# An attention that loads its values from the kernel's output, in place of a second copy sorted by head

## The chip, the cores and the metric

The kernel runs on one core of a Trainium2 chip. The core has five engines with queues of their own: TensorE (PE: matmuls, and PEld for its weight loads), VectorE (DVE), ScalarE (ACT), GpSimd (POOL) and SyncE (SP), which here issues nearly all transfers. 16 DMA engines carry them. The metric is the time of one execution on the device in microseconds (us).

## The reference, cut to what matters

One inference step of a decoder with two layers: a recurrent layer (RG-LRU), then a layer of forgetting attention. Between them the keys K, the values V and a log forget value are computed once from the residual stream `x`. Two groups go through it: a prompt of 2,048 new tokens, and 8 sequences of 8 new tokens each ("sample"), which also read 4,096 past tokens from a paged cache of K and V (32 pages of 128 tokens per sequence). There are 16 heads of 64, and `D_MODEL` is 1024.

```
z = rms_norm(x, kv_norm) @ w_kv
k, v = z[..., :1024], z[..., 1024:2048]        # both are outputs of the kernel, row by row
logf = log_sigmoid(z[..., 2048:] + b_f);  c = cumsum(logf)
...
zz = rms_norm(x, b_pre_norm) @ b_w_in;   q, g = zz[..., :1024], zz[..., 1024:]
s  = q k^T / 8 + c_q - c_k, causal;   o = softmax(s) v          # per head
x  = x + rms_norm((o * silu(g)) @ b_w_out, b_post_norm)
```

All is in float32. The outputs include `v_prompt`, of shape (1, 2048, 16, 64): a token's row holds its 16 heads one after the other.

## The kernel before, in words

The recurrent layer runs in two parts of 1,024 tokens, and the projections behind it (`phase_b`) in three: 64 sample rows and 1,024 prompt tokens, then 512, then 512. `phase_b` goes through kinds and column blocks in a written order (`B_ORDER`, `B_ENDS`, `B_LAST`): "k" and "v" are computed token by token (`token_major`: one tile is 128 tokens by 256 columns, that is four heads), "q" and "g" feature by feature (`feature_major`). Each float32 matmul is made of three (L386 to L388), high and low parts multiplied with each other; the weights are split into these parts on the way in (ACT L431, DVE L432).

A "v" tile `kf` goes out twice. L928 writes its 256 columns to the output `v_p` (`vp_flat` is the same memory as 2,048 rows of 1,024). L939 writes it again to `v_d`, a scratch tensor in DRAM laid out by head: [head, 128 tokens of a tile, tile, 64]. In this copy a head's values for one partition, 16 tiles of 64 floats, are 4 KB in one piece. A profile calls the scratch tensor `vd`, the weights before the split `wst`, and the activations `xh` and `xl`; the last two are read back from DRAM for the third part (L1943, `back`).

The attention of the prompt (`attention`) takes the heads one by one and each head's queries in four blocks of 512. A tick is one block of 128 keys: a score matmul in two halves (L1653, L1654), an exponential on ACT (L1664), and every four or eight ticks a `product` of the probabilities with the values (L1677). A head has 40 ticks. At tick 16 of a head the next head's keys and values are loaded (L1407, L1411), the values into one of two tiles, `vvs[0]` and `vvs[1]`. `vvs[0]` is a tile of its own (in the profile `vvt`); `vvs[1]` is the first quarter of the memory that held the low parts of the activations (`attl`). The rest of that memory holds tiles of queries and of row sums.

Beside `phase_b` and the attention runs the decode of the sample group (`decode`): for each sequence and half of the heads (a "turn") the 32 key pages are loaded (L1138, `raw`, 256 KB each), turned on VectorE (L1210), multiplied with the queries on PE (L1194), then the softmax, then the 32 value pages and their products (L1292). `Side` lays decode and main work side by side in the program by costs written down by hand. All these loads and stores stand in the one queue of SP, in order; the order within each engine's queue is worked out when the program is built, by a scheduler that uses simulated times (`schedule_with_timeline_sim`, L2007), with some places fixed by hand (`paged`, `behind`, `together`).

After the last head the output projection (`project`) takes tiles of 128 tokens: `fetch` loads the attention's output, the reciprocals of the row sums and the gate (`sg`, [128, 8, 128]), `gate` multiplies them in two halves (PE L1746, DVE, POOL L1748), then `split`, the matmuls, and `post`. Two sets of tiles take turns; the gate tile of the first set (`sgT`) is a tile of its own, that of the second lies in memory of a key tile.

Of the kernel before, what the change touches and what calls it, by code (L numbers as in the profile page):

```python
# [20 lines left out]
P = 128  # L21
D = 1024
KB = 8
# [65 lines left out]
def tile_hawk_fox(  # L89
# [80 lines left out]
    def dt_(name, shape):  # L170
        return dram.tile(shape, F32, name=name, tag=name)
# [9 lines left out]

    kd_d, qd_d = dt_("kd", [D, 2, SEQ]), dt_("qd", [D, 2, SEQ])
    sg_d = dt_("sgd", [D, SEQ])
    v_d = dt_("vd", [H, P, SEQ // P, HD])
    nc_d = dt_("ncd", [H, 3, SEQ])
    ks_d, vs_d = dt_("ksd", [NSAMP, D]), dt_("vsd", [NSAMP, D])

# [690 lines left out]
    def phase_b(s, x, feed, nk, early, order, opening=None):  # L878
# [7 lines left out]
        with ExitStack() as es:  # L886
# [22 lines left out]
            def token_major(kind, cc):  # L909

                nonlocal forget
                W = feed.take()
                isk = kind == "k"
                kfs = []
                w = WC if (kind, cc) == ("k", 0) else 256
                for i, (col, m, samp, tok) in enumerate(s.tiles):
                    ps = mmp("kv")
                    mm3(ps[:m, :w], lambda k: xh(k, col, m), lambda k: xl(k, col, m),
                        W.h(0, w), W.l(0, w), KB)
                    kf = pool.tile([P, 256], F32, name="kf", tag="kf", bufs=nk)  # L920
                    A.copy(kf[:m, :], ps[:m, :256])  # L921
                    if w > 256:
                        tt(V, s.z[:m, i, :], ps[:m, 256:w], bfB[:m, :], ALU.add)
                        if i == nt - 1 and not early:
                            forget = logf(s, pool)
                    sl = slice(cc * 256, (cc + 1) * 256)
                    dst = (ks_flat if samp else kp_flat[tok:tok + m]) if isk else (vs_flat if samp else vp_flat[tok:tok + m])
                    S.dma_start(dst[:, sl], kf[:m, :])  # L928
                    if samp:
                        S.dma_start((ks_d if isk else vs_d)[:, sl], kf[:m, :])  # L930
                        known.add((kind, cc))
                    elif isk:
                        kfs.append((kf, tok))
                        if len(kfs) == 4 or i == nt - 1:
                            for fb in range(2):
                                later.after(2 + fb, lambda grp=kfs, cc=cc, fb=fb: keys(grp, cc, fb))
                            kfs = []
                    else:
                        S.dma_start(v_d[cc * 4:cc * 4 + 4, :, tok // P, :].rearrange("h p d -> p h d"), kf[:, :].rearrange("p (h d) -> p h d", h=4))  # L939
                    later.tick()  # L940
                    if i == nt - 1 or i == 0:
                        feed.fetch()
                        feed.fetch()
                    if i >= 1:
                        feed.split()
                        feed.fetch()
                    next(forget, None)
                    yield 24 * 109
# [417 lines left out]
    def attention(es):  # L1366
# [41 lines left out]
            heads[h] = ka  # L1408

        def load_values(h):  # L1410
            S.dma_start(vvs[h % 2][:, :, :], v_d[h])  # L1411


        def load_unit(u):
# [161 lines left out]
        room = sbuf(es, "att2")  # L1576
        kbs.append(xs2[0][:, :SEQ])
        kas.append(xs2[0][:, SEQ:])
        vvs.append(f(xs2[1][:, :1024]).rearrange("p (k d) -> p k d", k=16))
        part = [xs2[1][:, i * 512:(i + 1) * 512] for i in range(2, 8)]  # L1580
        qbs.extend(part[:3])
        lent["rr"] = part[3:5]
        qal += [part[5], room.tile([P, 512], F32R, name="qa3")]

        def ring(tiles):
            turn_ = [0]
# [134 lines left out]
    def project(es):  # L1721

        bpostB, out = proj["g"], proj["out"]

        def tiled(t):
            return t.rearrange("p (k t) -> p k t", k=KB)

        def fetch(i, og, sg):
            m, t, res, _ = rows[i]
            if t is None:  # L1730
                tt(V, og[:, :, :m], oTs[:, :, :], sgs[:, :, :], ALU.mult)
                return
            qc, at = t // 512, slice(t % 512, t % 512 + P)
            S.dma_start(og[:, :, :], og_d[qc][:, at].rearrange("(k p) t -> p k t", p=P))
            for j, rr in enumerate(lent["rr"]):
                S.dma_start(f(rr[:4, :]).rearrange("z (k t) -> z k t", k=4),
                            r_d[qc, :, :, j * 4:(j + 1) * 4, at].rearrange("x z k t -> (x z) k t"))
            S.dma_start(sg[:, :, :], sg_d[:, t:t + P].rearrange("(k p) t -> p k t", p=P))

        def gate(i, og, sg):  # L1740
            if rows[i][1] is None:
                return
            for j, rr in enumerate(lent["rr"]):
                half = slice(j * 4, (j + 1) * 4)
                ps = lent["psum"].tile([P, 512], F32, name="rp", tag="sx", bufs=3)
                T.matmul(ps[:, :], sel[:, :], rr[:, :], start=True, stop=True)  # L1746
                tt(V, og[:, half, :], og[:, half, :], ps[:, :].rearrange("p (k t) -> p k t", k=4), ALU.mult)
                tt(G, og[:, half, :], og[:, half, :], sg[:, half, :], ALU.mult)  # L1748

        def residual(i, x1):  # L1750
            m, t, res, _ = rows[i]
            S.dma_start(x1[:m, :], res)

        def split(i, og, oh, ol):
            m = rows[i][0]
            cp(A, oh[:, :, :m], og[:, :, :m])
            tt(V, ol[:, :, :m], og[:, :, :m], f(oh[:, :, :m]), ALU.subtract)

        def post(i, yps, x1, y):
            m, t, res, dst = rows[i]  # L1760
            halves_ = [slice(j * 512, (j + 1) * 512) for j in range(2)]
            if i == len(rows) - 1:
                for sl, ps in zip(halves_, yps):
                    tt(V, y[:m, sl], ps[:m, :], bpostB[:m, sl], ALU.mult)
            ss = sumsq(None, yps, m)
            r = rsqrt(ss[:m], m, 0.25 / D, post=0.5)
            for sl, ps in zip(halves_, yps):
                if i == len(rows) - 1:
                    V.scalar_tensor_tensor(y[:m, sl], y[:m, sl], r[:m, 0:1], x1[:m, sl], op0=ALU.mult, op1=ALU.add)
                    S.dma_start(dst[:, sl], y[:m, sl])  # L1770
                else:
                    V.scalar_tensor_tensor(y[:m, sl], ps[:m, :], r[:m, 0:1], bpostB[:m, sl], op0=ALU.mult, op1=ALU.mult)
                    tt(G, y[:m, sl], y[:m, sl], x1[:m, sl], ALU.add)
            if i < len(rows) - 1:
                S.dma_start(dst, y[:m, :])

        pool = sbuf(es, "proje", "right")
        hs = lent["halves"]
        sel = pool.tile([P, P], F32R, name="selz")
        G.memset(f(sel[:, :]), 0.0)  # L1780
        for z in range(2):
            tt(V, sel[:4, z * HD:(z + 1) * HD], ident[:4, z:z + 1].to_broadcast([4, HD]),
               ident[:4, z + 2:z + 3].to_broadcast([4, HD]), ALU.add)
        sets = [dict(og=pool.tile([P, KB, P], F32, name="ogT"), sg=pool.tile([P, KB, P], F32, name="sgT"), x1=proj["x1"],
                     oh=pool.tile([P, KB, P], F32R, name="ohT"), ol=pool.tile([P, KB, P], F32R, name="olT"),
                     y=proj["y"],
                     ps=lambda j: psum["dec"].tile([P, 512], F32, name="y", tag="do"[j], bufs=1)),
                dict(og=tiled(lent["og"][:, :D]), sg=tiled(lent["res"][:, :D]), x1=lent["res"][:, D:], oh=tiled(hs[:, :D]), ol=tiled(hs[:, D:]),
                     y=lent["out"][:, :, :].rearrange("p k d -> p (k d)"),
                     ps=lambda j: lent["psum"].tile([P, 512], F32, name="y", tag="st", bufs=2))]  # L1790

        def part(i, fn, *names):
            if i < len(rows):
                fn(i, *(sets[i % 2][n] for n in names))

        for i in range(2):
            part(i, fetch, "og", "sg")
            part(i, residual, "x1")
        part(0, split, "og", "oh", "ol")
        for i in range(len(rows)):  # L1800
            b = sets[i % 2]
            yps = []
            part(i + 1, gate, "og", "sg")
            for j in range(2):
                ps = b["ps"](j)
                out.product(ps, rows[i][0], j, b["oh"], b["ol"])
                yps.append(ps)
                if j == 0:
                    part(i + 2, fetch, "og", "sg")
                    part(i + 1, split, "og", "oh", "ol")  # L1810
            post(i, yps, b["x1"], b["y"])
            part(i + 2, residual, "x1")
            if i == 3:
                later.flush()
# [203 lines left out]
```

## Time and profile before

| | us |
|---|---|
| median of 3 runs | 2939.27 |
| lowest and highest run | 2931.56, 2940.05 |
| the profiled execution | 2939.13 |
| its span, first to last instruction | 2937.4 |
| PE busy in it | 2749.3 (94%) |
| busy time of q1, the queue of nearly all transfers, as a share of 16 DMA engines | 68.1% |

The profile is of one execution. A group of instructions in it is one line of the program with what it writes and reads (`vd<-kf`); "x64" is the number of instructions. A wait is told as "who <- whom: us in total, times, longest". PE's busy time includes matmuls that are slow because the clock is held back, so the granted clock (PEclk) is read beside it. For DMA, a packet is one piece that lies together at both ends, and the busy share is that of 16 engines.

### The profile page before, as it was taken

Reading aid. Unit: us, or ns where it says so; the run is one execution under the profiler, and the core shown is the slowest. Engines: PE = TensorE matmul, PEld = TensorE weight load, DVE = VectorE, ACT = ScalarE, POOL = GpSimd, SP = SyncE. Lnnn points to the kernel's source line nnn. Section 1 sums busy time; section 2 is a strip of 40 time slices with the busy share of each in tenths; the row PEclk is TensorE's granted clock in tenths of the full one; section 3 lists DMA queues with packets and bytes.
Section 4 is the critical chain, followed back from the end, with each engine's and each line's share of the span. In section 5 each row is a group of like instructions: output and inputs, shape, how many; then the busy total and the mean of one; then the engine's idle time right before and its main releaser. Section 6 shows DMA issues by size and latency. Waiting matters only on the chain.

```text
span 2937.4 us, 59474 instructions
## 1 busy us (share of the span) xinstructions
PE 2749.3 (94%) x21086; PEld 2229.5 (76%) x21086; DVE 1814.4 (62%) x3971; ACT 1266.8 (43%) x2874; POOL 1099.7 (37%) x1207
## 2 busy tenths in 40 slices
PE   5998999999999999999999999899999999999998
PEld 5997789988898997897878666556666665556687
DVE  7877456344257774776564676766766765655465
ACT  4666342222245664533342344454444444356221
POOL 1654110000014552100001175656565565559554
PEclk9999999999999999999999999999999999999999
DMA  4224536789751246699999979978889877783453
GB/s 126 82 91 132 161 125 182 220 258 307 240 159 63 79 137 187 231 302 349 322 349 319 334 253 327 304 258 284 280 287 312 285 256 261 245 276 90 125 189 130
DMA packets 488149, 654.91 MB, mean 223 GB/s; under 512 B 93752, under 2 KB 288057, under 8 KB 480380
## 3 DMA queue, kind: packets, MB, share of 16 engines
q1 hardware_dynamic: 487564, 649.01, 68.1%
q8 instruction: 167, 2.74, 0.4%
q0 software_dynamic: 288, 2.10, 0.2%
q14 instruction: 130, 1.06, 0.1%
HBM read 514.87 MB, written 135.95 MB: 222 GB/s over the span
## 4 chain that ended last, share of the span: by engine, by line
PE 60%; DMA 15%; DVE 9%; ACT 6%; SPq 5%; issue 3%; POOL 1%; DVEq 0%; ACTq 0%; POOLq 0%
PE ops L1677 8%; PE st L1653 4%; PE sx L1440 4%; PE y L386 4%; PE y L388 4%; PE y L387 4%; DMA raw<-in_cache_k_dram 4%; PE st L1654 3%; PE dO L1292 3%; PE dS L1194 3%; DMA raw<-in_cache_v_dram 3%; PE qg L388 2%; PE qg L386 2%; PE qg L387 2%; SPq L1138 2%
## 5 line engine op out<-in xcount | busy, mean ns | idle before, releaser
L1210 DVE STREAM_TRANSPOSE ktr<-raw 128x1024 f32<-128x1024 f32 x256 | 308.1, 1226 | 107.8 <-DMA raw<-in_cache_k_dram 80.0
L1442 DVE TENSOR_REDUCE mxs<-sx 128x1 f32<-128x512 f32 x384 | 254.2, 681 | 145.3 <-PE sx L1440 144.3
L386 PE MATMUL kv<-wh,xh 128*128 128x256 f32 (+3 forms) x1088 | 310.3, 289 | 11.5 <-DMA xh<-xhd 4.6
L387 PE MATMUL kv<-wl,xh 128*128 128x256 f32 (+3 forms) x1088 | 309.6, 287 | 3.1 <-DVE wl L432 3.1
L388 PE MATMUL kv<-wh,xl 128*128 128x256 f32 (+3 forms) x1088 | 309.9, 287 | 0.8 <-DMA xl<-xld 0.8
L431 ACT ACTIVATE wh<-wst,gv 128x256 fp32r<-128x256 f32 (+1 forms) x384 | 164.3, 499 | 213.7 <-DMA wst<-in_b_w_in_dram 92.0
L432 DVE SCALAR_TENSOR_TENSOR wl<-wst,gv,wh 128x256 fp32r<-128x256 f32 (+1 forms) x384 | 171.0, 495 | 127.8 <-ACT wh L431 117.8
L386 PE MATMUL qg<-xh,wh 128*128 128x384 f32 (+2 forms) x640 | 229.9, 361 | 4.2 <-DVE qtl L965 4.1
L388 PE MATMUL qg<-xh,wl 128*128 128x384 f32 (+2 forms) x640 | 229.5, 360 | 1.0 <-DVE wl L432 1.0
L387 PE MATMUL qg<-xl,wh 128*128 128x512 f32 (+2 forms) x640 | 228.9, 359 | 0.0
L386 PEld LDWEIGHTS kv<-wh,xh 128*128 128x128 f32 (+1 forms) x1088 | 203.9, 189 | 17.1 <-issue 8.5
L387 PEld LDWEIGHTS kv<-wl,xh 128*128 128x128 f32 (+1 forms) x1088 | 204.0, 188 | 6.4 <-DVE wl L432 4.2
L388 PEld LDWEIGHTS kv<-wh,xl 128*128 128x128 f32 (+1 forms) x1088 | 205.1, 189 | 3.8 <-issue 2.4
L1158 POOL TENSOR_TENSOR qw<-qb,amask 128x128 f32<-128x128 f32 x64 | 25.8, 409 | 432.3 <-PE dS L1194 166.9
L1446 DVE CUSTOM_DVE_ANT_0 sx<-sx,maskb 128x128 f32<-128x128 f32 (+3 forms) x256 | 122.9, 489 | 94.4 <-PE sx L1440 87.3
L1664 ACT ACTIVATE attl<-st 128x512 f32<-128x512 f32 (+3 forms) x236 | 120.9, 523 | 115.6 <-PE st L1654 55.7
L1292 PE MATMUL dO<-raw,sx 128*32 128x256 f32 x2048 | 140.8, 397 | 28.7 <-DMA raw<-in_cache_v_dram 24.2
L1664 ACT ACTIVATE attw<-st 128x512 f32<-128x512 f32 (+3 forms) x224 | 119.0, 549 | 97.8 <-PE st L1654 59.9
L109 POOL TENSOR_TENSOR atth<-atth,attl 128x512 f32<-128x512 f32 (+3 forms) x119 | 127.1, 1070 | 79.8 <-ACT attl L1664 51.8
L109 POOL TENSOR_TENSOR atth<-atth,attw 128x512 f32<-128x512 f32 (+3 forms) x116 | 132.1, 1139 | 47.0 <-ACT attw L1664 32.2
L1664 ACT ACTIVATE atth<-st 128x512 f32<-128x512 f32 (+3 forms) x180 | 92.7, 522 | 125.2 <-PE st L1656 69.7
L921 ACT COPY kf<-kv 128x256 f32<-128x256 f32 (+1 forms) x136 | 48.9, 365 | 221.5 <-PE kv L388 174.5
(359 smaller groups left out, 7669.4 us busy)
## 6 DMA issues: line engine op xcount, KB each, us to landing
raw<-in_cache_k_dram SPq DMA_DIRECT2D x512, 256.0 KB
raw<-in_cache_v_dram SPq DMA_DIRECT2D x512, 256.0 KB
wst<-in_w_kv_dram SPq DMA_DIRECT2D x48, 512.0 KB
wst<-in_b_w_in_dram SPq DMA_DIRECT2D x48, 512.0 KB
xt<-in_x_prompt_dram SPq DMA_DIRECT2D x32, 512.0 KB
wst<-in_a_w_in_dram SPq DMA_DIRECT2D x64, 256.0 KB
out_dram<-kf SPq DMA_DIRECT2D x128, 128.0 KB
sc<-cd SPq DMA_DIRECT2D x16, 1024.0 KB
```

The costliest lines, as they stand in the source:

```text
L109: eng.tensor_tensor(out, a, b, op=op)
L386: T.matmul(ps, lh(k), rh(k), start=(k == 0), stop=False)
L387: T.matmul(ps, lh(k), rl(k), start=False, stop=False)
L388: end = T.matmul(ps, ll(k), rh(k), start=False, stop=(k == nk - 1))
L431: A.activation(wh[:, k, :], st[:, k, :], AF.Copy, scale=gk)
L432: V.scalar_tensor_tensor(wl[:, k, :], st[:, k, :], gk, f(wh[:, k, :]), op0=ALU.mult, op1=ALU.subtract)
L1210: behind("V", V.transpose(t.kts[pp][:, n], raw[:, :, pp * 256:(pp + 1) * 256]).ins)
L1292: return T.matmul(op[c:c + 32, :256], sx[:, d, i // 4, a * 4:(a + 1) * 4, :].rearrange("p h q -> p (h q)"), raw[:, d, a * 256:(a + 1) * 25 ...
L1442: r = V.reduce_max(mx[:, j, ck:ck + 1], ps[:, :w], axis=AX.X)
L1446: V.tensor_tensor_reduce(ps[:, :w], ps[:, :w], maskb[:, 512 - w:], scale=1.0, scalar=NEG, op0=ALU.add, op1=ALU.max, accum_out=mx[:, j, ck: ...
L1664: pair.append((k, lo, p, A.activation(p[:, lo:], ps[:, lo:], AF.Exp)))
L1677: return T.matmul(ops[r * HD:(r + 1) * HD, a0 * P:], vvs[h % 2][:, k, :], p[:, :].rearrange("p (a r c) -> p a r c", a=2, r=2)[:, a0:, r, : ...
```

## The change

The second copy of V is gone: the tensor `v_d` and the stores at L939. `load_values` reads a head from the output itself: for each of 128 partitions 16 pieces of 64 floats (256 bytes), 128 rows apart.

The other edits move tiles. `vvs[1]` becomes a tile of its own (4 KB in each partition). In return the fourth tile of the ring `qal` goes to the memory that `vvs[1]` left, and so does half of the first set's gate tile, whose own tile shrinks to half. For that the gate is loaded, and used, as two tiles of four blocks in both sets.

```
-    v_d = dt_("vd", [H, P, SEQ // P, HD])
...
-                    else:
-                        S.dma_start(v_d[cc * 4:cc * 4 + 4, :, tok // P, :].rearrange("h p d -> p h d"), kf[:, :].rearrange("p (h d) -> p h d", h=4))
...
         def load_values(h):
-            S.dma_start(vvs[h % 2][:, :, :], v_d[h])
+            S.dma_start(vvs[h % 2][:, :, :], vp_flat[:, h * HD:(h + 1) * HD].rearrange("(k p) d -> p k d", p=P))
...
         room = sbuf(es, "att2")
...
-        vvs.append(f(xs2[1][:, :1024]).rearrange("p (k d) -> p k d", k=16))
+        vvs.append(room.tile([P, 16, HD], F32, name="vvt1"))
...
-        qal += [part[5], room.tile([P, 512], F32R, name="qa3")]
+        qal += [part[5], xs2[1][:, :512]]
+        lent["sg"] = f(xs2[1][:, 512:1024])
...
-        def tiled(t):
-            return t.rearrange("p (k t) -> p k t", k=KB)
+        def tiled(t, k=KB):
+            return t.rearrange("p (k t) -> p k t", k=k)
...
-            S.dma_start(sg[:, :, :], sg_d[:, t:t + P].rearrange("(k p) t -> p k t", p=P))
+            for j in range(2):
+                S.dma_start(sg[j], sg_d[j * 512:(j + 1) * 512, t:t + P].rearrange("(k p) t -> p k t", p=P))
...
-                tt(G, og[:, half, :], og[:, half, :], sg[:, half, :], ALU.mult)
+                tt(G, og[:, half, :], og[:, half, :], sg[j], ALU.mult)
...
-        sets = [dict(og=..., sg=pool.tile([P, KB, P], F32, name="sgT"), x1=proj["x1"],
+        sets = [dict(og=..., sg=[pool.tile([P, 4, P], F32, name="sgT")[:, :, :], tiled(lent["sg"], 4)], x1=proj["x1"],
...
-                dict(og=..., sg=tiled(lent["res"][:, :D]), x1=lent["res"][:, D:], ...
+                dict(og=..., sg=[tiled(lent["res"][:, j * 512:(j + 1) * 512], 4) for j in range(2)], x1=lent["res"][:, D:], ...
```

More of the change, by code (lines that the diff above doesn't have):

```diff
@@ L1783, in project @@
                ident[:4, z + 2:z + 3].to_broadcast([4, HD]), ALU.add)
-        sets = [dict(og=pool.tile([P, KB, P], F32, name="ogT"), sg=pool.tile([P, KB, P], F32, name="sgT"), x1=proj["x1"],
+        sets = [dict(og=pool.tile([P, KB, P], F32, name="ogT"), sg=[pool.tile([P, 4, P], F32, name="sgT")[:, :, :], tiled(lent["sg"], 4)], x1=proj["x1"],
                      oh=pool.tile([P, KB, P], F32R, name="ohT"), ol=pool.tile([P, KB, P], F32R, name="olT"),
@@ L1787, in project @@
                      ps=lambda j: psum["dec"].tile([P, 512], F32, name="y", tag="do"[j], bufs=1)),
-                dict(og=tiled(lent["og"][:, :D]), sg=tiled(lent["res"][:, :D]), x1=lent["res"][:, D:], oh=tiled(hs[:, :D]), ol=tiled(hs[:, D:]),
+                dict(og=tiled(lent["og"][:, :D]), sg=[tiled(lent["res"][:, j * 512:(j + 1) * 512], 4) for j in range(2)], x1=lent["res"][:, D:], oh=tiled(hs[:, :D]), ol=tiled(hs[:, D:]),
                      y=lent["out"][:, :, :].rearrange("p k d -> p (k d)"),
```

## The prediction, made before the changed kernel was run

> **What bounds the kernel now.** I read the page first, then a table of stages, then the two tensors that the change touches, then the waits of TensorE (PE) in the stages where those tensors move.
>
> From the page: the engines' busy time, and the clock and DMA rows over the span's 40 slices.
> ```profile
> span 2937.4 us, 59474 instructions
> PE 2749.3 (94%) x21086; PEld 2229.5 (76%) x21086; DVE 1814.4 (62%) x3971; ACT 1266.8 (43%) x2874; POOL 1099.7 (37%) x1207
> DMA  4224536789751246699999979978889877783453
> ```
> PE is busy for 94% of the span, so a transfer matters only where PE stands still for it. The DMA digits are 9 in slices 18 to 23 (about 1250 to 1690 us) and 7 to 9 in the twelve or so after that: before the attention the DMA engines are full, in it they have a little room. The table of stages puts the two side by side.
> ```profile
> core 0: us, PE busy (x) PEld busy (x) DVE busy (x) ACT busy (x) POOL busy (x), PEclk, DMA share, GB/s
> 560.00:640.00 80.00, 76.72 (x843) 75.93 (x841) 39.60 (x68) 21.62 (x64) 1.71 (x5) 1.00 0.90 265
> 700.00:770.00 70.00, 66.47 (x734) 64.38 (x734) 34.35 (x61) 19.42 (x57) 0.24 (x1) 0.98 0.86 252
> 1260.00:1320.00 60.00, 57.93 (x661) 55.55 (x660) 43.43 (x74) 21.34 (x59) 1.70 (x5) 1.00 1.01 319
> 1400.00:1440.00 40.00, 34.58 (x275) 32.07 (x274) 17.44 (x44) 15.13 (x46) 0.00 (x0) 0.91 1.02 330
> 1440.00:1570.00 130.00, 118.45 (x1036) 99.86 (x1036) 79.30 (x162) 44.24 (x113) 1.70 (x5) 0.93 1.00 336
> 1570.00:1640.00 70.00, 70.00 (x684) 62.62 (x683) 30.34 (x53) 20.68 (x52) 12.76 (x19) 1.00 1.00 317
> 1640.00:1700.00 60.00, 54.57 (x427) 39.44 (x425) 42.18 (x98) 24.31 (x67) 19.77 (x24) 0.94 0.99 329
> 1700.00:2690.00 990.00, 930.07 (x8415) 606.16 (x8415) 657.83 (x1370) 471.86 (x1165) 606.85 (x582) 0.97 0.82 272
> 2690.00:2937.00 247.00, 237.31 (x1106) 181.20 (x1104) 137.01 (x323) 64.03 (x140) 131.65 (x98) 0.98 0.43 135
> ```
> The stretches up to 1440 us and 1570 to 1640 are those with value stores, 1700 to 2690 is the attention with the decode beside it, the last is the output projection. Length less PE busy is what can be won in a stretch at all: 3.3, 3.5, 2.1, 5.4, 11.6, 0.0 and 5.4 us before the attention, and a clock below 1.00 adds to it (0.91 over 40 us is 3.6 us).
>
> **The change part by part.** The view of the tensor `vd` shows what goes and what stays.
> ```profile
> L939 SPq DMA_DIRECT2D vd<-kf x64: 370/427/1481, 572.8 to 1635.0; - x64
> L1411 SPq DMA_DIRECT2D vvt<-vd x8: 319/434/1215, 1645.7 to 2585.0; - x8
> L1411 SPq DMA_DIRECT2D attl<-vd x8: 319/404/430, 1699.6 to 2637.3; - x8
> ```
> *Removed: 64 stores* (L939). Each writes 128 KB in 512 packets of 256 bytes (128 tokens, 4 heads of 64 floats). The price of such a packet I take from half a microsecond in which nothing else moved, and beside it one in which 256-byte packets were read, and two microseconds of 4-KB packets:
> ```profile
> DMA packets 430, 0.11 MB, mean 220 GB/s; under 512 B 430, under 2 KB 430, under 8 KB 430
> q1 hardware_dynamic: 430, 0.11, 95.7%
> ```
> ```profile
> DMA packets 427, 0.11 MB, mean 217 GB/s; under 512 B 427, under 2 KB 427, under 8 KB 427
> q1 hardware_dynamic: 427, 0.11, 92.9%
> ```
> ```profile
> DMA packets 117, 0.48 MB, mean 240 GB/s; under 512 B 0, under 2 KB 0, under 8 KB 117
> q1 hardware_dynamic: 117, 0.48, 65.3%
> ```
> The last column is the share of 16 engines. So a 256-byte store takes 0.957 x 16 x 500 / 430 = 17.8 ns, a 256-byte read 0.929 x 16 x 500 / 427 = 17.4 ns, a 4-KB packet 0.653 x 16 x 2000 / 117 = 179 ns. One store holds the 16 engines for 512 x 17.8 / 16 = 0.57 us, all 64 for 36.5 us: 16 each (9.1 us) in 560 to 640, 700 to 770 and 1570 to 1640, 8 each (4.6 us) in 1260 to 1320 and 1400 to 1440. SP is also spared 64 issues of 427 ns, in a queue in which pages and weights stand behind them.
>
> What of this reaches PE? The waits of PE in the first two of these stretches, and then in 1400 to 1440:
> ```profile
> PE dS L1194 <- DVE ktr L1210: 3.3, 2, 2.4
> ```
> ```profile
> PE kv L387 <- DVE wl L432: 2.2, 1, 2.2
> PE dS L1194 <- DVE ktr L1210: 1.3, 1, 1.3
> ```
> ```profile
> PE kv L386 <- DMA xh<-xhd: 4.6, 2, 4.3
> PE kv L388 <- DMA xl<-xld: 0.8, 2, 0.5
> ```
> VectorE's L1210 turns a page that has just come, and L432 splits a weight that has just come; in a stretch with 0.86 to 0.90 DMA share both are late because the queue is. With 9.1 us less in the queue I let 3.0 of the 3.3 and 3.0 of the 3.5 us go (bounds 0, and all of it with B's clock, 4.9). For 1260 to 1320 I take 0.5 of 2.1, since no store stands ahead of most of it. In 1400 to 1440 the activations are read back (L1943) and PE waits for them; SP's queue, in order, shows what stands ahead:
> ```profile
> 1404.98 0.42 SPq L939 DMA_DIRECT2D vd<-kf  x1
> 1408.71 0.45 SPq L939 DMA_DIRECT2D vd<-kf  x1
> 1411.04 1.48 SPq L939 DMA_DIRECT2D vd<-kf  x1
> 1413.82 0.37 SPq L939 DMA_DIRECT2D vd<-kf  x1
> 1417.06 0.38 SPq L1943 DMA_DIRECT2D xh<-xhd  x1
> ```
> Four stores are 2.3 us of DMA time and 2.7 us of SP. I take 2.5 us off the wait of 4.3. PE then comes back on a slow clock, and its next matmul shows it:
> ```profile
> 1424.02 0.57 PE L386 MATMUL kv<-wh,xh 128*128 128x272 f32 x1 [4.32 <-DMA xh<-xhd]
> ```
> Of the 3.6 us that the 0.91 costs I take 1.0 back. (The Trainium skill, "TensorE: Matmul & The Clock Gate", Part 1, says that the clock halves after an idle window of about 3.4 us and comes back after as long a busy one. By that a wait cut below 3.4 us would return all 3.6, and the sum below would be lower by 2.6.)
>
> Of 1570 to 1640 nothing is won: PE is busy for 70.00 of 70. But the queue is full there, and the stall after it (1640 to 1700, 5.4 us idle and 3.6 us of clock) follows 16 stores; I take 3.0 (bounds 0 and 9.0). For 1440 to 1570, without a store, I take 0 (bound 4.6, what the stores before it held). Gain: 3.0 + 3.0 + 0.5 + 3.5 + 3.0 = **13.0 us**, bounds about 1 and 30.
>
> *Changed: 16 loads* (L1411). Before, 128 packets of 4 KB: 128 x 179 / 16 = 1.43 us of the 16 engines. After, 2,048 of 256 bytes: 2048 x 17.4 / 16 = 2.23 us. That is 0.80 us more, 12.8 us for 16, of which 14 (11.2 us) run beside pages of the decode. The value itself isn't late: PE's stops ahead of the products (L1677) name ACT, and no load.
> ```profile
>   issue: 20.9, 77
>   ACT attl L1664: 6.4, 13
> ```
> Who pays are the pages behind the load in SP's queue. In the attention:
> ```profile
> PE dO L1292 <- DMA raw<-in_cache_v_dram: 20.3, 10, 6.8
> ```
> ```profile
> 2233.77 8.08 DMA attl<-vd
> ```
> The second row is from the chain of waits: there a value load, 8.08 us from issue to landing, holds the pages. PE's idle time in 1700 to 2690 is 59.9 us, and 20.3 of it, a third, is named to pages; so I let a third of 11.2 us through: **4 us** (bounds 0 and 11.2, with the 18% of free DMA time speaking for the lower end).
>
> Do the pieces lie badly? A head's 16 pieces of a partition lie 128 rows of 4 KB apart, 512 KB. The removed stores had that spacing too (a head of `vd` is 128 x 4 KB), and ran at 17.8 ns, against 17.4 for reads from a dense tensor. (The Trainium skill, "DMA: Bandwidth & Descriptors", Latency and other measured facts, speaks against the change: copies whose partitions lie 512 KiB apart ran at 207 GB/s. An estimate from it is 2.5 us a load in place of 2.23, 4 us more over 14 loads if all of it showed. The trace's 17.8 ns does not bear it out for stores; no run so far shows it for loads.)
>
> *Order of reading.* Head 0's load now follows the output's stores, the last of which is issued next to the last `vd` store at 1635.0; at 1645.7 it has landed or holds SP for 1 to 2 us, 44 us ahead of its use. I take 0.
>
> *Moved tiles.* The second value tile takes memory that the last gate products held until their stores, and the fourth tile of the ring of query rows goes to the memory of the old activations, where its neighbours lie already.
> ```profile
> L984 SPq DMA_DIRECT2D sgd<-tgb x38: 319/332/2003, 763.8 to 1689.6; - x38
> L1738 SPq DMA_DIRECT2D sgT<-sgd x8: 374/387/392, 2660.9 to 2886.7; - x8
> ```
> The last such store is issued at 1689.6, the first load into the tile at 1699.6: 10 us, enough even for an 8-us landing; 0, bounds 0 and 3. In the projection 16 gate loads become 32 of half the size: 16 more issues of 0.39 us, 6.2 us of SP in 247 us, with PE busy for 237.31 of them; 0, bounds -1 (a half can be fetched when its first half is used up) and 6 without that cover.
>
> **Sum.** -13.0 + 4 = -9 us. The profiled execution took 2939.13 us (span 2937.4), the median of the runs 2939.27, the same for this purpose: 2930.
>
> **Rivals.** *The stalls only move* (no change, 0.37). PE's work in each stretch is in order, and VectorE and ACT are late for other reasons too; a page that comes 2 us earlier may meet the next late weight. For it: PE lost 11.6 us in 1440 to 1570, where no store is. Then 13 shrinks to about 5, less 4 for the loads: 2938, and anything from 2931 to 2948.
> *The loads hold up the pages* (slower, 0.20). Place: SP's queue from 1700 to 2590, pages behind 2,048 packets. Price: if reading at this spacing goes at half the rate, a load takes 4.46 us, 3.03 more than now; 14 loads are 42 us, two thirds of it through, 28, less the 13: 2954. It outweighs the gain from 13 / 14 = 0.93 us a load on that PE feels; 0.3% slower starts at 1.56. Against it: the stores' 17.8 ns, and that only a third of PE's idle time there is for pages. Even at 0.80 us a load with everything through and a gain of 2 it is 2948.
> *The queue is laid out anew.* The order in each queue is worked out by a scheduler from simulated times (L2007), so 64 transfers fewer may put a page elsewhere; one stop for a page is up to 6.8 us (row above), either way. That lies inside the range and the other chances.
>
> **How the numbers follow.** 0.3%, 8.8 us, is about what a measurement of this kernel tells from no change. Forecast (relief counts, loads mostly hidden): 0.43, from 2930 down to 2909 with all bounds at once. Range: 2912 (27 us of the 30 without any cost, about 1 in 20 below) to 2952 (short of the doubled load; about 1 in 8 above). The likeliest case alone spans 2912 to 2930.
>
> **What would show it.** No `vd` store; written bytes down by 8.4 MB; PE's wait for `xh` near 1420 at about 2 us in place of 4.3; fewer stops at L1194 in 560 to 770; DMA share down in these stretches and 1 to 2% up in 1700 to 2690; packets of a value load near 17 to 18 ns. Wrong would be: stops of PE of the same sum before 1700 us, or PE's wait for value pages well over 20 us with loads that take 4 us or more.

## The result and the profile after

The changed kernel takes 2962.3 us (median of 4 runs, 2959.99 to 2967.87), the kernel before beside it 2936.6: a ratio of 1.0063, 95% interval 1.0037 to 1.0089. It is slower by 0.63% (18.5 us of 2936.6; the two medians lie 25.7 us apart, inside the interval), and lies above the range of the forecast. The profiled execution took 2963.84 us.

The page of the changed kernel: span and busy time, the DMA row over 40 slices, the bytes.
```profile
span 2961.8 us, 59444 instructions
PE 2760.7 (93%) x21086; PEld 2229.9 (75%) x21086; DVE 1812.2 (61%) x3971; ACT 1266.0 (43%) x2874; POOL 1096.7 (37%) x1207
DMA  4224536769741246699999979977889888773363
HBM read 514.87 MB, written 127.56 MB: 217 GB/s over the span
```
The change does what it says: 8.4 MB fewer are written (127.56 MB in place of 135.95). Yet PE is 11 us longer busy and 13 us longer idle. Where, a table of stages shows. The two executions reach the same work at different times, so each is cut at its own marks: 560 us, a point in the first gate projection (`qg`, the same matmul in every run, called "the gates" from here on), the first and the last product of scores and values (`ops`), the end. The kernel before, then the changed one, with the columns of the table in the prediction (stretch, length, busy time of PE, PEld, DVE, ACT, POOL, clock, DMA share, GB/s):
```profile
560.00:771.00 211.00, 199.62 (x2089) 190.28 (x2087) 89.11 (x154) 55.60 (x156) 1.95 (x6) 0.98 0.89 272
771.00:1690.00 919.00, 868.49 (x6389) 773.68 (x6389) 562.78 (x1210) 403.75 (x883) 182.23 (x267) 0.98 0.73 238
1690.00:2739.00 1049.00, 989.07 (x8852) 643.34 (x8850) 675.50 (x1415) 500.92 (x1233) 650.88 (x622) 0.97 0.78 261
```
```profile
560.00:787.00 227.00, 208.52 (x2159) 196.26 (x2158) 89.84 (x156) 57.97 (x161) 1.95 (x6) 0.97 0.82 256
787.00:1686.00 899.00, 858.50 (x6273) 768.23 (x6272) 556.97 (x1204) 403.62 (x883) 180.59 (x267) 0.98 0.70 231
1686.00:2764.00 1078.00, 1002.01 (x8921) 643.58 (x8921) 680.77 (x1422) 500.13 (x1233) 651.83 (x622) 0.97 0.79 256
```
Up to the gates it is 16 us longer although the DMA engines have less to do (0.82 against 0.89), then 20 shorter, and in the attention 29 longer. The number of matmuls (the x behind PE busy) shows that these stretches do not hold the same work: 70 more up to the gates, 116 fewer behind them, 69 more in the attention. So a second mark is of use, the start of the next block of key and value projections (`kv`), by which every run but e1, e2 and e4 has done the same 7,464 matmuls: the kernel before reaches it at 1199.4 us, the changed kernel at 1209.1. Two views point at causes.

The first is SP's queue around a value load, of the kernel before and of the changed one (start, duration of the issue, line, what is moved):
```profile
2091.30 0.32 SPq L1411 DMA_DIRECT2D attl<-vd  x1
2092.23 0.34 SPq L1138 DMA_DIRECT2D raw<-in_cache_v_dram  x1
2092.66 0.62 SPq L1485 DMA_DIRECT2D ogd<-attw  x1
```
```profile
1979.30 0.43 SPq L1404 DMA_DIRECT2D atth<-kd  x1
1979.78 0.43 SPq L1408 DMA_DIRECT2D vvt<-out_dram  x1
1980.32 4.59 SPq L1482 DMA_DIRECT2D ogd<-attw  x1
```
The load itself is issued in 0.43 us. The next DMA of that queue takes 4.59 us to issue, where 0.3 to 0.8 is usual. Of the issues that begin within 1.5 us behind a value load, the longest takes 0.32 to 0.82 us before and 3.6 to 10.0 us after, at every one of the 16 loads; over the whole span SP has no issue of over 3 us before and 16 after, one behind each load. I call it the hold.

The second is what SP and PE waited for in the stretch ahead of the gates (who <- whom: us in total, times, longest), of the kernel before, then of the changed one:
```profile
SPq L928 <- ACT kf L921: 9.0, 7, 1.9
```
```profile
PE dS L1194 <- DVE ktr L1210: 4.6, 3, 2.4
```
```profile
SPq L927 <- ACT kf L920: 26.9, 13, 9.0
```
```profile
PE dS L1191 <- DVE ktr L1207: 10.2, 4, 5.1
```
With 64 stores fewer to place, the scheduler put the instructions of every engine into another order: from the first missing store on the queues differ, and one output store now holds SP for 9 us with four key pages behind it.

### The profile page after: what moved, and what is told of

The parts are those of the page before. It is cut to its first block, busy times and chain, and to the rows that moved or that the text cites. A ratio compares the mean times of both kernels' runs of the same rounds, so it can differ in the third digit from the quotient of the medians.

```text
span 2961.8 us, 59444 instructions
## 1 busy us (share of the span) xinstructions
PE 2760.7 (93%) x21086; PEld 2229.9 (75%) x21086; DVE 1812.2 (61%) x3971; ACT 1266.0 (43%) x2874; POOL 1096.7 (37%) x1207
## 3 DMA queue, kind: packets, MB, share of 16 engines
HBM read 514.87 MB, written 127.56 MB: 217 GB/s over the span
## 4 chain that ended last, share of the span: by engine, by line
PE 60%; DMA 16%; DVE 9%; ACT 6%; SPq 4%; issue 3%; POOL 2%; DVEq 0%; ACTq 0%; POOLq 0%
PE ops L1675 7%; PE y L385 4%; PE y L387 4%; PE y L386 4%; PE st L1651 4%; DMA raw<-in_cache_k_dram 4%; PE dO L1289 3%; DMA raw<-in_cache_v_dram 3%; PE sx L1437 3%; PE qg L385 3%; PE qg L386 3%; PE qg L387 3%; PE st L1652 3%; PE dS L1191 3%; PE kv L385 3%
## 5 line engine op out<-in xcount | busy, mean ns | idle before, releaser
L1207 DVE STREAM_TRANSPOSE ktr<-raw 128x1024 f32<-128x1024 f32 x256 | 307.7, 1226 | 123.9 <-DMA raw<-in_cache_k_dram 107.3
L1289 PE MATMUL dO<-raw,sx 128*32 128x256 f32 x2048 | 146.9, 409 | 36.6 <-DMA raw<-in_cache_v_dram 25.2
L1191 PE MATMUL dS<-ktr,qw 128*32 128x128 f32 x4096 | 128.6, 280 | 18.4 <-DVE ktr L1207 15.9
```

The costliest lines, as they stand in the source:

```text
L1191: return T.matmul(sp[a * 32:(a + 1) * 32, h * P:(h + 1) * P], qw[:, pp * 2 + h // 2, h % 2 * 2 + x, :], kt[:, :, a, blk:blk + 32], start=( ...
L1207: behind("V", V.transpose(t.kts[pp][:, n], raw[:, :, pp * 256:(pp + 1) * 256]).ins)
L1289: return T.matmul(op[c:c + 32, :256], sx[:, d, i // 4, a * 4:(a + 1) * 4, :].rearrange("p h q -> p (h q)"), raw[:, d, a * 256:(a + 1) * 25 ...
```

## The experiments

Theories: **order** (the new static order costs the time), **load** (the 256-byte loads hold up the pages), **tiles** (a moved tile makes somebody wait). To part work from order, a kernel can be tied to a list: each instruction depends, for its place only, on the one that stands ahead of it in the list on the same engine.
```
         tile_hawk_fox(tc, *args)
+        keep_order(tc)
...
+        if e in last:
+            tc.add_manual_dep(i, last[e].name, ORDER)
+        last[e] = i
```
Ratios below are to runs of the kernel before on the same chip, with 95% intervals; 0.001 is 2.9 us.

**A false start.** In e1, e2 and e4 (e3, the new loads without the moved tiles, has no time) the list was not the scheduler's, as I had believed, but the order in which the program is written.

> The changed kernel's work, all of it (no value stores, 256-byte value loads, moved tiles), but each engine's instructions are tied to stand in the order in which the kernel before has them (the stores left out of the row). Order theory (the 64 stores left the static order that the scheduler laid out, and the new order costs the 26 us): 2925 to 2940 us, near the 2930 of the forecast's sum. Load theory (the value loads in 256-byte packets hold up the pages): the loads are all here, so 2955 to 2970. Tile theory (a moved tile makes somebody wait): also 2955 to 2970.

> The work of the kernel before, all of it (64 value stores, 4-KB value loads, tiles unmoved), but each engine's instructions are tied to stand in the order of the changed kernel, each value store right behind the store of its key-and-value tile. Order theory: as slow as the changed kernel or slower by what the stores cost, 2958 to 2975 us. Load theory and tile theory: nothing of what they blame is in it, so 2932 to 2945.

> The kernel before in its own order, with its value stores and its 4-KB loads, but with the tiles moved as in the change (one value tile, one query tile, half a gate tile, gate loads as two halves). Order theory and load theory: within 4 us of the kernel before, 2933 to 2941 us. Tile theory: 2955 to 2970.

Measured: 1.5199 (1.5163 to 1.5234), 1.5244 (1.5213 to 1.5275), 1.5228 (1.5199 to 1.5258), some 4480 to 4490 us. All three ran in the order of the text, so the expectations do not apply, and nothing follows on the theories. What it does show: the order alone is worth 1540 us here.

**Work against order.** The same three, tied to the orders that the scheduler made.

> The changed kernel's work, all of it, with each engine's instructions tied to the order into which the scheduler put the kernel before (e1 to e4 had tied them to the order of the program text, which is another). Order theory: 2925 to 2940 us, near the 2930 of the forecast's sum. Load theory and tile theory: 2955 to 2970, since every load and every moved tile is in it.

> The work of the kernel before, all of it, with each engine's instructions tied to the order into which the scheduler put the changed kernel, each value store right behind the last instruction that SP has ahead of it in the program. Order theory: as slow as the changed kernel or slower by what the stores cost, 2958 to 2975 us. Load theory and tile theory: 2932 to 2945.

> The kernel before in its own scheduled order, with its value stores and its 4-KB loads, and with the tiles moved as in the change. Order theory and load theory: within 4 us of the kernel before; this is also the control for the tying itself. Tile theory: 20 us or more above the kernel before.

Measured: e5 1.0031 (1.0015 to 1.0047), e6 1.0073 (1.0054 to 1.0093), e7 0.9995 (0.9978 to 1.0012). The tile theory is out, and e7 shows that the tying costs nothing. No theory has e5: counted from 2937 us, the order theory said 0.996 to 1.001 and the load theory 1.006 to 1.011, and it lies between them. e6 is at the lower edge of what the order theory said (1.007 to 1.013): with all the work of before, the new order costs 0.0078 against e7, 23 us. The stages of e7, e5 and e6, one after the other, say where (up to the gates; then the attention):
```profile
558.00:769.00 211.00, 202.64 (x2126) 193.71 (x2125) 90.09 (x156) 58.11 (x161) 3.43 (x10) 0.99 0.91 278
769.00:1694.00 925.00, 869.25 (x6388) 773.59 (x6386) 562.43 (x1209) 402.96 (x882) 181.34 (x267) 0.98 0.72 236
1694.00:2741.00 1047.00, 982.56 (x8851) 639.89 (x8851) 675.63 (x1415) 501.37 (x1232) 650.63 (x622) 0.98 0.78 261
```
```profile
557.00:764.00 207.00, 202.00 (x2120) 193.06 (x2120) 90.10 (x156) 58.11 (x161) 2.73 (x9) 0.99 0.84 263
764.00:1674.00 910.00, 864.54 (x6386) 771.05 (x6384) 558.94 (x1209) 403.12 (x882) 181.94 (x267) 0.98 0.71 236
1674.00:2749.00 1075.00, 991.10 (x8854) 644.09 (x8852) 672.95 (x1416) 500.73 (x1233) 650.87 (x622) 0.97 0.79 254
```
```profile
558.00:797.00 239.00, 214.15 (x2170) 201.03 (x2169) 90.02 (x156) 58.37 (x161) 3.39 (x10) 0.95 0.85 262
1716.00:2770.00 1054.00, 995.46 (x8914) 640.92 (x8914) 678.09 (x1420) 498.65 (x1231) 649.58 (x621) 0.97 0.78 262
```
In the order of before, the missing stores bring 20 us ahead of the attention (it starts at 1674 in place of 1694), and the attention, with the new loads, takes 28 us more (1075 against 1047). In the new order with the old loads the attention is nearly as short as before (1054), but the gates come 28 us late. Part of the 28 us is work done earlier (44 matmuls more than e7 up to there); at the mark of 7,464 matmuls e6 is 24 us late (1221.8 against 1198.1). So both theories hold, each in its own stage.

**What of the load costs?** Either its packets, or the hold.

> The changed kernel's work in the scheduled order of the kernel before, as in e5, but the 16 value loads are issued by ACT and not by SP; same 256-byte packets. In e5 the stretch ahead of the attention was 20 us shorter than in e7 and the attention 28 us longer (first to last ops matmul, 1047 against 1075 us), and the DMA that SP issues behind each value load took 4 to 10 us to issue in place of some 0.5. Hold theory (SP is held at that issue, and pages come late by it): attention 1045 to 1055 us, ratio 0.990 to 0.996. Packet theory (the 256-byte packets cost the DMA engines 19.9 ns each, 41 us for 32768 of them, against 22 us for the 4-KB packets, and the attention lasts as long as its DMA work): attention 1065 to 1080, ratio 1.000 to 1.005.

> As e5 (no value stores, tiles moved, scheduled order of the kernel before), but each value load reads 128 dense rows of 4 KB from another array, so that the packets are those of before and the values are other numbers. Hold theory and packet theory: attention 1045 to 1052 us, start of the attention at 1670 to 1680, ratio 0.991 to 0.996; it is what the missing stores are worth with loads at the price of before. If the missing stores themselves or the moved tiles slow the attention: 1065 to 1080 still.

> As e5, but each value load is cut into four of 512 packets, one every fourth step of the head and a page or more between them; the same 256-byte packets in all. Hold theory: each hold is a quarter and hidden by the pages under way, attention 1048 to 1062 us, ratio 0.992 to 0.999. Packet theory: as e5 within 5 us, attention 1070 to 1080.

> As e10, but each value load in two of 1024 packets, eight steps of the head apart. What e10 and e9 leave (ratio 0.9959 in quarters, 0.9927 with dense loads, 1.0031 whole in e5) is split by how the hold grows. A hold that grows with the packets (about 3 us behind each half, twice as many): near half way from e10 to e5, 0.998 to 1.002. A hold that begins only above some number of packets, and a half is below it: as e10, 0.994 to 0.997; SP then shows no issue over 3 us more than before has.

The edits, each on top of e5 (the loads of e8, e10 and e11 find their own place in the queue, everything else keeps its place; e9, e10 and e11 replace the line that e8 takes out):
```
e8   -S.dma_start(vvs[h % 2][:, :, :], vp_flat[:, h * HD:(h + 1) * HD]...)
     +A.dma_start(vvs[h % 2][:, :, :], vp_flat[:, h * HD:(h + 1) * HD]...)
e9   +S.dma_start(vvs[h % 2][:, :, :], kd_d[h % 8 * P:(h % 8 + 1) * P, 0, :1024].rearrange("p (k d) -> p k d", d=HD))
e10  +S.dma_start(vvs[h % 2][:, q * 4:q * 4 + 4, :], vp_flat[q * 512:(q + 1) * 512, h * HD:(h + 1) * HD]...)
...
     +            if k in (16, 20, 24, 28) and h + 1 < H:
     +                with paged():
     +                    load_values(h + 1, k // 4 - 4)
e11  as e10, two loads of 1024 rows, at k in (16, 24)
```
Measured: e8 1.0000 (0.9984 to 1.0015), e9 0.9927 (0.9904 to 0.9951), e10 0.9959 (0.9944 to 0.9975), e11 0.9962 (0.9949 to 0.9975). The attention of e9 and of e10:
```profile
1679.00:2728.00 1049.00, 982.93 (x8853) 640.36 (x8849) 677.81 (x1415) 500.99 (x1233) 650.98 (x622) 0.98 0.78 260
```
```profile
1673.00:2731.00 1058.00, 984.38 (x8855) 639.61 (x8854) 676.10 (x1416) 501.83 (x1233) 652.14 (x622) 0.97 0.80 258
```
With dense loads it takes 1049 us, with all the 256-byte packets in quarters 1058, with the same packets in one piece 1075. So the packets cost some 9 us (ratios: 0.0032, with intervals that overlap; the 48 more issues of the quarters are in it too), and that they come in one piece 17 us more (ratios: e5 less e10, 0.0072, 21 us). The hold theory has e10, and both theories have e9. SP's queue around a load in e5, in e11 and in e10:
```profile
2090.74 0.40 SPq L1408 DMA_DIRECT2D vvt<-out_dram  x1
2091.78 5.56 SPq L1135 DMA_DIRECT2D raw<-in_cache_v_dram  x1
```
```profile
2089.40 0.40 SPq L1408 DMA_DIRECT2D vvt<-out_dram  x1
2090.43 1.71 SPq L1135 DMA_DIRECT2D raw<-in_cache_v_dram  x1
```
```profile
2091.60 0.43 SPq L1408 DMA_DIRECT2D vvt<-out_dram  x1
2092.23 0.52 SPq L1414 DMA_DIRECT2D qbt<-qd  x1
```
Behind 2048 packets the page's issue takes 5.56 us, behind 1024 it takes 1.71, behind 512 a usual 0.52. Over all loads, the longest issue within 1.5 us takes 3.8 to 9.5 us in e5, 0.3 to 6.9 in e11 (mostly under 2.4), 0.3 to 1.7 in e10 and 0.3 to 1.1 in e9. Issues of over 3 us in the whole span: 16 in e5, 3 in e11, none in e10, e9 and e8. Halves cost no more than quarters, so the price does not grow evenly with the packets: e11's time is as the second case of its expectation has it, though that case allowed no issue of over 3 us. That short holds are hidden and one of six us is not would fit it, but isn't shown. Nor is it shown through which of PE's waits the hold costs its 17 us. PE waits for value pages 22.8 us in e5's attention and 27.2 in e10's, where the hold is gone; its whole idle time falls from 84 to 74 us, and its busy time by 7.

e8 fits neither theory whole: its ratio is at the packet theory's lower edge, its attention, 1059 us, lies between the two. The loads keep their packets and their one piece, and none of SP's issues takes over 3 us; so the attention's 16 us go with the hold on SP, not with the burst of packets. But the loads now stand in ACT's row, and PE waits for ACT (e5 first, then e8, in the attention):
```profile
PE st L1651 <- ACT attl L1662: 7.1, 18, 1.4
```
```profile
PE st L1651 <- ACT attl L1662: 20.1, 18, 8.6
```
One more such stop, of 6.9 us, lies just ahead of it. The trace shows where they come from, and it is not the hold: ahead of four of the 16 loads ACT stands for 2.5 to 8.9 us, by the trace until a transfer issued by SP has landed (pages, `sgd`, `ogd`), and then issues the load; the activations stand behind it. (The Trainium skill, "DMA: Bandwidth & Descriptors", Issuing engines are not separate DMA queues, says that another issuing engine saves only the sequencer's time, usually a small one. Here the time saved on SP was not small: the longest issue behind a load took 3.8 to 9.5 us in e5, at most 0.6 in e8.)

**The order with the hold gone.** The quarters in the changed kernel's order, and with nothing tied.

> The value loads in quarters as in e10, everything else tied to the scheduled order of the changed kernel. The hold (0.0072 between e5 and e10) goes and the order's price stays (0.0073 in e6 with the work of before; changed kernel 1.0063 in its own order, 1.0031 in that of before): 0.997 to 1.003, attention 1055 to 1065 us. If hold and order are one thing, so that without the hold the order costs nothing: 0.994 to 0.997. If the changed kernel's loss is in its order alone: 1.004 to 1.008.

> The changed kernel with its value loads in quarters and nothing tied: the scheduler makes an order of its own once more. The work is that of e10, 0.9959 in the order of before; an order was worth 3 to 21 us so far (e6 against e7, the changed kernel against e5), either way unknown, so 0.992 to 1.005. In the attention, without the hold: 1050 to 1066 us.

Measured: e12 1.0005 (0.9993 to 1.0017), e13 0.9978 (0.9961 to 0.9995). Against e10 the order costs 0.0046 with this work, 14 us, so hold and order are two things. Three orders of the same work lie between 0.9959 and 1.0005; e13's, within what was expected, is the one that the scheduler makes by itself.

**Where the order costs.** e12 reaches the gates at 783 us, e10 at 763; at the mark of 7,464 matmuls it is 1204.4 against 1189.3. The plainest suspect was the store in SP's queue.

> As e12 (quarters, scheduled order of the changed kernel), but at one place of SP's queue, near 592 us, four key pages stand ahead of the output store that in e12 waits there for ACT's copy until 601 us, and of the two stores behind it. In e12 the pages are issued from 603.2 us on, and near there PE stops 5.6 us for the transposed page (L1207). Order theory with its price in this queue: that stop is gone or under 2 us, 4 to 9 us less with the clock that follows a stop, ratio 0.9975 to 0.9990. If the pages find no free buffer before 601 us, or something else is late next: the stop stays within 1.5 us of 5.6, ratio 1.000 to 1.001.

The edit changes the list of SP alone: four page loads, then the two output stores and the store between them. Measured: 1.0004 (0.9988 to 1.0019), as e12. SP's waits up to the gates in e12 and in e14:
```profile
SPq L927 <- ACT kf L920: 26.9, 14, 7.1
...
SPq L1135 <- DVE ktr L1207: 4.4, 3, 2.0
```
```profile
SPq L927 <- ACT kf L920: 15.8, 11, 2.5
SPq L1135 <- DVE ktr L1207: 10.0, 4, 5.5
```
The store no longer holds SP, but now the pages do: they wait up to 5.5 us for the transposes (L1207) to empty a buffer. PE's one stop there, of 5.6 us, became two, of 5.5 us together, and the time stayed: the second case of the expectation. So that place is a sign of the order's price, not its source. The last two runs cut the order at the gates.

> The work of e10 (value loads in quarters) in a mixed order: what the kernel before has put ahead of the first gate projection (about 771 us) stands in the order of the changed kernel, all the rest in that of the kernel before. e10 (all in the order of before) has 0.9959, e12 (all in the order of the changed kernel) 1.0005. If the order's price arises ahead of 771 us, as the traces show it (e12 reaches the gates 20 us after e10): 0.999 to 1.004. If it arises behind: 0.995 to 0.9975.

> The reverse of e15: the order of the kernel before up to the first gate projection, that of the changed kernel behind it. If the order's price arises ahead of 771 us: 0.992 to 0.997, with the gates reached by 770 us. If it arises behind, in the attention above all: 0.999 to 1.003.

Measured: e15 1.0026 (1.0008 to 1.0044), e16 0.9995 (0.9981 to 1.0008). e15 is as the first case has it: the first part of the new order is enough for the loss. With the same 4,952 matmuls done, its first gate matmul starts at 771 us, e10's at 750. e16's ratio lies in the range of the second case, which would speak against e15, but its trace does not have the loss in the attention. It keeps the old order up to the cut, starts its first gate matmul at 754 us, and loses right behind it: the stretch from 738 to 780 us takes 14 us longer than e10's from 735 to 763. In it PE waits 7.4 us for value pages, which in e10 it does not, the granted clock is 0.88 against 1.00, and 48 products of the decode's values are done that come later in e10:
```profile
PE dO L1289 <- DMA raw<-in_cache_v_dram: 7.4, 3, 5.8
```
From the mark of 7,464 matmuls to the last product e10 takes 1541.6 us, e12 1540.8, e15 1543.0, e16 1538.0. So behind that mark the new order costs nothing, and its price arises ahead of it: from 2,710 matmuls (near 530 us) to 7,464 it is 13 us in e12 and 16 in e15, and e15 has all of it ahead of the gates. e16's loss comes at the seam between two orders, which neither whole order has. Which of the moved instructions starts the price stays open.

## Why the prediction was wrong, step by step

*64 stores removed, -13.0 us.* Right in kind, too small. e9 less e7, 0.9927 against 0.9995, is 20 us for the missing stores; in the traces of e7 and e5 the attention begins 20 us sooner, of which 4 are won up to the gates (forecast 6.0) and 15 behind them (7.0). In the order of before, PE's waits at L1210 and L432 are gone from the list up to the gates, as forecast (one of 3.2 us for another transfer has come). PE's wait for `xh` near 1420 is gone in e5. In the changed kernel it is 2.5 us (forecast about 2, before 4.3), as the line shows; but e7, with all 64 stores, has 2.4, so that number alone does not speak for the forecast:
```profile
PE kv L385 <- DMA xh<-xhd: 2.5, 1, 2.5
```
*16 loads, +4.* This step failed, and most of the miss is here. e5 less e9 is 0.0104, 31 us. Two things were wrong in it. "A third of 11.2 us let through" was a guess from the share of PE's idle time that pages are named for; e10 less e9 shows some 9 us, most of it, as far as two overlapping intervals tell. And the hold, 21 us, is not in the sum at all: I had priced the load by the time of its packets, and asked who waits for the load, but not what its 2,048 packets do to the next issue of SP. The 8.08 us of one old value load, quoted in the prediction, was a landing time, and said nothing of that. The packet itself was a little dearer than the 17.4 ns. Two microseconds of e5 in which nearly all packets are such:
```profile
DMA packets 1638, 0.52 MB, mean 259 GB/s; under 512 B 1625, under 2 KB 1625, under 8 KB 1625
...
q1 hardware_dynamic: 1638, 0.52, 109.7%
```
That is 1.097 x 16 x 2000 / 1638 = 21.4 ns a packet (the share adds up the packets' times, and passes 100% here), but 13 of them are of 8 KB. The 256-byte packets alone took 19.2 ns there, and 19.9 ns as the mean of the 15 loads in e5's attention: 2.5 us a load, 1.1 more than before. In quarters (e10) the mean is 18.2 ns, 2.3 us a load. (The estimate from the Trainium skill's rule of the 512 KiB pitch, "DMA: Bandwidth & Descriptors", Latency and other measured facts, was 2.5 us. It fits the loads in one piece, but may do so by chance: the rule is of partitions that lie 512 KiB apart, here the pieces of one partition do and the partitions lie 4 KB apart, and the quarters, with the same spacing, are cheaper. No run parts spacing from packet size.)

*The loads hold up the pages*, the rival on the slow side, had the right place, SP's queue, and nearly the right sum (28 us through, and 2954). Its route was another: it asked for packets at half the rate, so that the sum is near is luck. What I held against it, the price of a packet, is no argument against a hold.

*Moved tiles, 0.* Right: e7 is 0.9995. *Order of reading, 0*: not tried alone (e9 reads another array). In e5, which has it, the first load is issued at 1627.7 us and first used at 1674.

*The queue is laid out anew.* Named as a rival, and said to be worth up to 6.8 us either way. It was worth 23 us with the work of before (e6 against e7), 14 with the loads in quarters (e12 against e10), 9 with the loads whole (1.0063 against e5's 1.0031; these two intervals overlap). I had sized it as one stop for one page. But an order shifts many small things, and a longer stop brings a slower clock: in e6 PE waits 16.7 us for transposed pages up to the gates, with stops of up to 5.8 us, at a granted clock of 0.95 against e7's 0.99. With each of e6's five stops of 3.2 to 5.8 us in that stretch the granted clock falls to 0.50 for 3.4 or 6.8 us; with one of 1.4 us it does not.
```profile
PE dS L1194 <- DVE ktr L1210: 16.7, 4, 5.8
```
(That agrees with the rule of the Trainium skill that the prediction weighed, "TensorE: Matmul & The Clock Gate", Part 1: idle windows above about 3.4 us halve the clock. Here a stop of 3.2 us was enough.)

So the sum as measured, in ratios from e7 on: stores -0.0068 (e9), packets +0.0032 (e10), hold +0.0072 (e5), order +0.0032 (the changed kernel), together +0.0068, and 0.9995 + 0.0068 = 1.0063. Each term is the step from one run to the next, so that they add up is no test of them; the packets and this order are the two that the intervals hardly part from nothing. Of the forecast's own signs of being wrong, the first came true: PE's idle time from 560 us to the attention is 59 us, before 62. The second came in part: loads that hold SP for 4 us and more did, but PE's wait for value pages in the attention is only 24.9 us, against 20.3 before and 27.2 in the faster e10:
```profile
PE dO L1289 <- DMA raw<-in_cache_v_dram: 24.9, 15, 4.1
```
A kernel that beats both is at hand: the change with its loads in quarters, 0.9978 as the scheduler orders it, and 0.9959 in the order of before (0.9962 in halves).

## What to carry to other kernels

Price a DMA three times: by the time of its packets, by who waits for its data, and by what stands behind it in its queue; a load of 2,048 small pieces was cheaper here as two or four DMAs with other work between them. Where a scheduler lays out a static order, any edit buys a new one; tie the new work to the old order, and the old work to the new, before the edit is praised or blamed. And look at the stage in which a gain was forecast by its own marks, at which both kernels have done the same work: here the stores' 20 us were won, and covered by two losses.

## What the runs showed of the hardware that was not expected

An issue on SP took 3.6 to 10 us when a DMA of 2,048 packets had gone into the same queue shortly before, mostly under 2.4 behind 1,024, at most 2.1 behind 512 (e10, e12, e13) and at most 1.2 behind 128 packets of 4 KB (before, e6, e7, e9). Read packets of 256 bytes took 19.9 ns on average in loads of 2,048 and 18.2 in loads of 512, beside other transfers, against 17.4 ns where a few hundred ran alone. The same work in another order was 23 us slower in 2940 (e6 against e7), and five orders of the work with quartered loads spread over 20 us (e10, e12, e13, e15, e16).
